# The head of a decoder layer: unused products on TensorE, transposes by row tile, first tokens on VectorE

## The chip, the cores and the metric

The kernel runs on one core of one Trainium2 chip. TensorE (PE) multiplies matrices, VectorE (DVE), ScalarE (ACT) and GpSimd (POOL) do the rest, and SyncE (SP) issues most of the transfers. The metric is the time of one execution in device microseconds (us); several runs are made and their median counts.

## The reference, cut to what matters

One layer of a conditioned hybrid decoder, for 256 prompt tokens of one sequence and 64 sample tokens (eight sequences of eight). Both groups share every weight. The model has 2048 channels. All arithmetic is float32.

```python
mod = jax.nn.silu(c) @ w_ada + b_ada                      # one vector per sequence, 6 x 2048
sh1, sc1, g1, sh2, sc2, g2 = [m[:, None, :] for m in jnp.split(mod, 6, axis=-1)]
h = _rmsnorm(x, norm1_g) * (1 + sc1) + sh1
p = h @ w_in                                              # q, k, v, og, u, ga, gb, alr
...
x = x + g1 * (merged @ w_o)
h2 = _rmsnorm(x, norm2_g) * (1 + sc2) + sh2
gate, up = jnp.split(h2 @ w_gu, 2, axis=-1)
x = x + g2 * ((jax.nn.silu(gate) * up) @ w_down)
```

Nothing of `p` can be computed for a block of 128 channels before that block of `h` exists, and `h` needs x with its channels on the partitions, the reciprocal norm of each token, and the shift and scale (`sh1`, `sc1`) that come from a product of the conditioning vectors with the first third of `w_ada`.

## The kernel before, in words

Tokens lie along the free dimension: T = 320 columns, 256 prompt and 64 sample. Channels lie on the partitions, 16 blocks of 128 (KT = 16), called token tiles below: `xT[k]` is x of block k, `hh[k]` and `hl[k]` the rounded and the remaining part of h. Every weight goes through the same steps: a transfer from memory into a tile `raw` (line 142, three buffers), a rounded copy `whi` on ScalarE (152) and the remainder `wlo` on VectorE (153), and three products for each 128 x 128 block (166 to 168: whi with hh, whi with hl, wlo with hh).

The transfers of weights are issued on SyncE's queue, each pinned behind what was issued before it in the program (`keep_in_program_order` at 144). A queue whose next transfer waits for a buffer holds up all behind it. Other instructions are ordered by a scheduler that works from its own simulation, except where a line pins one behind the instruction traced before it on the same engine.

The head, in the order of the program:

- The conditioning vectors (nine rows) and x are loaded. x comes in three row tiles `xn[0..2]`: 128 + 128 prompt tokens and 64 sample tokens (lines 382 to 388). Small vectors come by GpSimd's queue (392 to 397).
- TensorE transposes the conditioning rows (400; `tr` is line 129), ScalarE and VectorE make silu of them, `scT`.
- For each of the 16 channel blocks three transposes, one from each row tile, fill one PSUM tile, which VectorE or ScalarE copies to `xT[k]` in turn (453 to 462).
- The squares of x are summed on ScalarE (476); a small product on TensorE spreads the reciprocal norm over all partitions, `rx` (478 to 486).
- `HeadJob` computes shift and scale for some channel blocks. Its `load` brings two tiles of `w_ada` (eight buffers), its `burst` multiplies them (`ada_mm`, line 218: four products side by side for each of four channel blocks), its `finish` transposes the result and adds the bias into `mod` (438 to 445, 233, 236). The first job makes them for token tiles 0 and 1 in four bursts.
- `h_unit(k)` makes hh[k] and hl[k]: VectorE works on the prompt columns (490, 497), GpSimd on the sample columns (491 to 493), ScalarE rounds (494, 495).
- The channel blocks are taken in slices (0 to 1, 2 to 3, 4 to 7, 8 to 11, 12 to 15). For each slice all units of the first head and some gates are projected: q, k, v (a pair of 256 columns), u, og, ga, gb and two further gb pairs. Between the units the next slice's work is spread as a list of steps: the spill of xT to memory by GpSimd's queue (503), the next HeadJob's load, its bursts and finish, and its h_units. `proj` (172) loads four blocks of 256 columns at a time, `proj_pair` (199) two blocks of 512.

After the slices the other three heads, the output projection and the feed-forward follow; the change touches nothing of these.

Of the kernel before, what the change touches and what calls it, by code (L numbers as in the profile page):

```python
# [11 lines left out]
F32 = mybir.dt.float32  # L12
F32R = mybir.dt.float32r
I32 = mybir.dt.int32
AF = mybir.ActivationFunctionType
ALU = mybir.AluOpType
# [4 lines left out]
P = 128  # L21
TP, NB, LS = 256, 8, 8
TS = NB * LS
T = TP + TS
D = 2048
KT = D // P
# [10 lines left out]
WB = 5  # L37
AB = 3
SLICES = ((0, 2), (2, 4), (4, 8), (8, 12), (12, 16))
# [41 lines left out]
def body(tc, A):  # L81
# [3 lines left out]
    wp = ctx.enter_context(tc.tile_pool(name="wp", bufs=3))  # L85
# [3 lines left out]
    hp = hcx.enter_context(tc.tile_pool(name="hp", bufs=1, side="right"))  # L89
    acx = ExitStack()  # L90
    pmain = ctx.enter_context(tc.tile_pool(name="pmain", bufs=2, space=PSUM))
# [5 lines left out]
    def nm(s):  # L97
        uid[0] += 1
        return "%s_%d" % (s, uid[0])

    def misc():
        return pmisc.tile([P, 512], F32, tag="m", name=nm("pm"))

    V, S, G, PE = nc.vector, nc.scalar, nc.gpsimd, nc.tensor
# [4 lines left out]
    ident = cst[:, 0:P]  # L109
    ones = cst[:, P:2 * P]  # L110
# [16 lines left out]
    def tr(out, in_):  # L127
        k = in_.shape[0]
        PE.transpose(out, in_, ident[:k, :k])  # L129
# [5 lines left out]
    def raw_chunk(src, nk, nn, pool=None, tag="raw", bufs=3):  # L135

        if pool is None and more:
            more.reverse()
            if more[0] is not None:
                pool, bufs = more[0], 2  # L140
        t = (pool or wp).tile([P, nk, nn], F32, tag=tag, bufs=bufs, name=nm("raw"))
        ins = nc.sync.dma_start(t, src)
        if in_order[0]:
            tc.keep_in_program_order(ins)
        return t
# [7 lines left out]
        V.tensor_sub(lo, raw, hi.bitcast(F32))  # L153
        return hi, lo

    def split_chunk(src, nk, nn):

        raw = raw_chunk(src, nk, nn)
        step = 512 // nn
        for k in range(0, nk, step):  # L160
            hi, lo = split(raw[:, k:min(k + step, nk)])
            for j in range(hi.shape[1]):
                yield k + j, hi[:, j], lo[:, j]
# [6 lines left out]
    def proj(w, col, k0, k1, xh, xl):  # L170

        ps = pmain.tile([P, 2, 512], F32, tag="pm", name=nm("ps"))
        for c0 in range(k0, k1, 4):
            nk = min(4, k1 - c0)
            for j, whi, wlo in split_chunk(w[:, c0:c0 + nk, col:col + 256], nk, 256):
                kt = c0 + j
                for i in range(2):
                    mm3(ps[:, i, :T], whi[:, i * P:(i + 1) * P], wlo[:, i * P:(i + 1) * P],
                        xh[kt], xl[kt], kt == k0, kt == k1 - 1)
            ada_pump()  # L180
        return ps
# [14 lines left out]

    def proj_pair(w, col, k0, k1, xh, xl):

        parts = list(split_chunk(w[:, k0:k1, col:col + 512], k1 - k0, 512))
        for half in range(2):  # L200
            ps = pmain.tile([P, 2, 512], F32, tag="pm", name=nm("ps"))
            for j, whi, wlo in parts:
                kt = k0 + j
                for i in range(2):
                    c = (2 * half + i) * P
                    mm3(ps[:, i, :T], whi[:, c:c + P], wlo[:, c:c + P], xh[kt], xl[kt], kt == k0, kt == k1 - 1)
            yield ps

    wada = A["w_ada"][0].rearrange("(kt p) n -> p kt n", p=P)
    win = A["w_in"][0].rearrange("(kt p) n -> p kt n", p=P)  # L210
# [79 lines left out]
    def modp(sec, kt):  # L290
        return mod[:, sec * KT + kt, 0:1]

    def mods(sec, kt):
        return mod[:, sec * KT + kt, 1:9].unsqueeze(2).broadcast_to([P, NB, LS])

    def s3(ap):
        return ap.rearrange("p (b t) -> p b t", t=LS)

    hh = [hp.tile([P, T], F32R, tag="hh%d" % k, name="hh%d" % k) for k in range(KT)]
    hl = [None] * KT  # L300
# [70 lines left out]
    def units(h):  # L371
        return [("q", 0, OQ + DK * h), ("k", 0, OK_ + DK * h), ("v", 0, OV + DV * h),
                ("v", 1, OV + DV * h + 256), ("u", 0, OU + 256 * h),
                ("og", 0, OOG + DV * h), ("og", 1, OOG + DV * h + 256),
                ("ga", 0, OGA + DV * h), ("ga", 1, OGA + DV * h + 256),
                ("gb", 0, OGB + DV * h), ("gb", 1, OGB + DV * h + 256)]


    with tc.tile_pool(name="head", bufs=1) as xp:
        junk = xp.tile([P, D], F32, name="junk")  # L380
        crow = junk[0:9, :]
        nc.sync.dma_start(crow[0:1, :], A["c_prompt"])
        nc.sync.dma_start(crow[1:9, :], A["c_sample"])
        xn = [xp.tile([P, D], F32, name="xn%d" % i) for i in range(3)]
# [9 lines left out]
        for j, n in enumerate(("norm1_g", "norm2_g", "final_norm_g", "pool_scale")):  # L394
            a = A[n] if n == "final_norm_g" else A[n][0]
            nc.gpsimd.dma_start(vr1[16 * j:16 * j + 16, :], a.rearrange("(r p) -> r p", p=P))
        nc.gpsimd.dma_start(vr1[64:68, :], A["gla_norm_g"][0].rearrange("(r p) -> r p", p=P))
        pt = misc()
        for k in range(KT):
            tr(pt[:, 16 * k:16 * k + 9], crow[:, k * P:(k + 1) * P])  # L400
        csig = xp.tile([P, KT, 9], F32, name="csig")
        crT = pt[:, 0:256].rearrange("p (k r) -> p k r", r=16)[:, :, 0:9]
        S.activation(csig, crT, AF.Sigmoid)
# [5 lines left out]
        class HeadJob:  # L409


            def __init__(self, b0, s):
                self.b0, self.s, self.w, self.nk = b0, s, 64 * s, 8 // s
                self.ps = None
                self.raws = {}
# [34 lines left out]


        xT = []
        for k in range(KT):
            pt = misc()
            for i in range(3):
                n = P if i < 2 else TS
                tr(pt[:, i * P:i * P + n], xn[i][:n, k * P:(k + 1) * P])
            if k < SLICES[0][1]:
                xT.append(xp.tile([P, T], F32, name="xT%d" % k))
            else:  # L460
                xT.append(hp.tile([P, T], F32, tag="hl%d" % k, name="xT%d" % k))
            (S.copy if k % 2 else V.tensor_copy)(xT[k], pt[:, 0:T])

        pt = misc()
        tr(pt[:, 0:96], vr0)
        tr(pt[:, 96:164], vr1)
# [2 lines left out]
        for sec in (1, 4):  # L469
            V.tensor_scalar(bada[:, sec * KT:(sec + 1) * KT], bada[:, sec * KT:(sec + 1) * KT], 1.0, None, op0=ALU.add)  # L470

        ssq = xp.tile([P, 3], F32, name="ssq")
        V.memset(ssq, 1.0)
        for i in range(3):
            n = P if i < 2 else TS
            S.activation(junk[:n], xn[i][:n], AF.Square, accum_out=ssq[:n, i:i + 1])
        S.activation(ssq, ssq, AF.Sqrt, scale=1.0 / D, bias=epst)
        V.reciprocal(ssq, ssq)
        prs = misc()
        dg = xp.tile([P, 3, P], F32, name="dg")  # L480
        for i in range(3):
            n = P if i < 2 else TS
            V.tensor_scalar(dg[:n, i, :n], ident[:n, :n], ssq[:n, i:i + 1], None, op0=ALU.mult)
            PE.matmul(prs[:, i * P:i * P + n], lhsT=ones[:n, :], rhs=dg[:n, i, :n], start=True, stop=True)
        rx = xp.tile([P, T], F32, name="rx")
        V.tensor_copy(rx, prs[:, 0:T])

        def h_unit(k):
            t = xp.tile([P, T], F32, tag="xh", bufs=2, name=nm("xh"))
            V.scalar_tensor_tensor(t[:, 0:TP], xT[k][:, 0:TP], modp(1, k), rx[:, 0:TP], op0=ALU.mult, op1=ALU.mult)  # L490
            G.tensor_tensor(t[:, TP:T], xT[k][:, TP:T], rx[:, TP:T], op=ALU.mult)
            G.tensor_tensor(s3(t[:, TP:T]), s3(t[:, TP:T]), mods(1, k), op=ALU.mult)
            G.tensor_tensor(s3(t[:, TP:T]), s3(t[:, TP:T]), mods(0, k), op=ALU.add)
            S.activation(hh[k][:, 0:TP], t[:, 0:TP], AF.Identity, bias=modp(0, k))
            S.copy(hh[k][:, TP:T], t[:, TP:T])
            hl[k] = hp.tile([P, T], F32R, tag="hl%d" % k, name="hl%d" % k)
            V.scalar_tensor_tensor(hl[k][:, 0:TP], t[:, 0:TP], modp(0, k), hh[k][:, 0:TP].bitcast(F32),
                                   op0=ALU.add, op1=ALU.subtract)
            V.tensor_sub(hl[k][:, TP:T], t[:, TP:T], hh[k][:, TP:T].bitcast(F32))  # L499
# [25 lines left out]
        for h in EARLY_GB:  # L525
            ge = G0()
            ge.gb = merged[h]
            early += [(ge, "gb", i, OGB + DV * h + 256 * i) for i in range(2)]
        for f in HeadJob(0, SLICES[0][1]).steps():
            f()  # L530
        for k in range(SLICES[0][1]):
            h_unit(k)
        for si, (k0, k1) in enumerate(SLICES):
            bg = []
            acc = 0 if si == 0 else 1
# [28 lines left out]
            e = 0  # L564
            while e < len(early):
                ge, kind, i, col = early[e]
# [445 lines left out]
    for ui in range(8):  # L1012
# [4 lines left out]
        for i in range(2):  # L1017
            residual(ps, i, 2 * ui + i, 2)
            k = 2 * ui + i
# [20 lines left out]
    for k in range(KT):  # L1040
        t = f2.tile([P, T], F32, tag="h2", bufs=3, name=nm("h2"))
# [6 lines left out]
                               op0=ALU.add, op1=ALU.subtract)  # L1048
# [4 lines left out]
    parts = ((0, 22), (22, 44))  # L1053
    ada_rate(0.75, 48)
    for pi, (f0, f1) in enumerate(parts):
# [22 lines left out]
        for ui in range(8):  # L1078
            ps = proj(wdn, 256 * ui, f0, f1, ah, al)
            for i in range(2):  # L1080
                k = 2 * ui + i
                residual(ps, i, k, 5)
                if pi == 1:
# [3 lines left out]
                    pt = misc()  # L1087
                    for a in range(3):
                        n = P if a < 2 else TS
                        tr(pt[:n, a * P:(a + 1) * P], xg[:, a * P:a * P + n])  # L1090
                    for a in range(3):
                        n = P if a < 2 else TS
# [5 lines left out]
    pt = misc()  # L1098
    for a in range(3):
        n = P if a < 2 else TS  # L1100
        PE.matmul(pt[:n, 2 * a:2 * a + 2], lhsT=acc2[:, a * P:a * P + n], rhs=ones[:, 0:2], start=True, stop=True)
    rr = fp.tile([P, 64], F32, name="rr")[:, 0:6]
    for a in range(3):
        n = P if a < 2 else TS
# [3 lines left out]
    for a in range(3):  # L1108
        n = P if a < 2 else TS
# [30 lines left out]
```

## Time and profile before

| | |
|---|---|
| median of three runs | 1993.09 us (1992.62 to 1994.77) |
| the profiled execution | 1993.81 us |
| its span, first to last instruction | 1992.0 us |
| granted TensorE clock, mean over the span | 0.991 |
| transfers | 400.83 MB, mean 201 GB/s |
| chain that ended last, by engine | TensorE 93%, transfers 4% |

The profile is one execution. Its timeline has rows of "start, duration, engine, line, operation, written tile and read tiles, shapes, count", merged where the same instruction repeats; brackets hold the idle time of the engine before it and what ended it. PEld are the weight loads of TensorE, which overlap with its products. A view of stretches gives for each the busy time of PE, PEld, DVE, ACT and POOL with the number of instructions, the granted clock, the share of the DMA engines' time and the rate. A view of transfers gives the count, the size of each and the time from issue to landing.

### The profile page before, as it was taken

The numbers are of one execution on the slowest core, as the hardware profiler recorded it, in microseconds if no ns is written. First come the engines' busy times: TensorE is split into PE (matmuls) and PEld (weight loads), VectorE is DVE, ScalarE is ACT, GpSimd is POOL, SyncE is SP. The second block draws the span as 40 slices with busy tenths as digits, with TensorE's granted clock in tenths as the row PEclk, the third lists the DMA queues.
The fourth block names the chain that finished last, engine by engine and source line by source line (L and its number), as shares of the span: only waits on it lengthen the run. The fifth ranks groups of instructions, "written<-read, shape, count | busy, mean of one in ns | idle before, by whom it ended". The sixth has DMA issues, their size and how long they took to land.

```text
span 1992.0 us, 37175 instructions
## 1 busy us (share of the span) xinstructions
PE 1942.7 (98%) x15008; PEld 1848.6 (93%) x15008; DVE 1014.1 (51%) x1881; ACT 819.6 (41%) x1468; POOL 137.5 (7%) x261
## 2 busy tenths in 40 slices
PE   7999999999999999999989999999999999999997
PEld 5789998898999899889979999999999999999997
DVE  2556665574546544664574444344444444444554
ACT  4333374364335333643353333343333434344443
POOL 1112220111011100110030000000000000000000
PEclk9999999999999999999989999999999999999998
DMA  9888754775975787579636666544445544444442
GB/s 296 287 303 271 230 165 147 263 262 187 325 245 174 269 266 234 167 248 339 226 112 223 202 221 193 167 150 143 156 147 151 153 152 148 149 148 149 148 143 90
DMA packets 319598, 400.83 MB, mean 201 GB/s; under 512 B 13529, under 2 KB 259801, under 8 KB 319089
## 3 DMA queue, kind: packets, MB, share of 16 engines
q1 hardware_dynamic: 307154, 358.21, 56.1%
q0 software_dynamic: 12272, 40.25, 5.4%
q8 instruction: 117, 1.92, 0.4%
q14 instruction: 55, 0.45, 0.1%
HBM read 373.96 MB, written 24.67 MB: 200 GB/s over the span
## 4 chain that ended last, share of the span: by engine, by line
PE 93%; DMA 4%; DVE 1%; ACT 1%; issue 1%; SPq 0%; POOL 0%; ACTq 0%; POOLq 0%; DVEq 0%
PE ps L166 27%; PE ps L168 27%; PE ps L167 27%; PE pm L218 5%; PE pm L129 2%; DMA raw<-w_ada 1%; DMA raw<-w_in 1%; DMA raw<-w_o 1%; PE pm L804 1%; PE pm L825 1%; PE pm L773 1%; DMA xn<-x_sample 1%; PE pm L800 0%; PE pm L762 0%; DVE wlo L153 0%
## 5 line engine op out<-in xcount | busy, mean ns | idle before, releaser
L153 DVE TENSOR_TENSOR wlo<-raw,whi 128x512 fp32r<-128x512 f32 x952 | 658.6, 696 | 817.5 <-ACT whi L152 807.5
L152 ACT CAST whi<-raw 128x512 fp32r<-128x512 f32 x952 | 586.3, 621 | 995.4 <-PE ps L167 843.8
L166 PE MATMUL ps<-hh,whi 128*128 128x320 f32 x1408 | 443.3, 315 | 6.5 <-ACT whi L152 3.0
L166 PE MATMUL ps<-h2h,whi 128*128 128x320 f32 x1408 | 437.4, 311 | 5.1 <-ACT h2h L1046 5.1
L168 PE MATMUL ps<-hh,wlo 128*128 128x320 f32 x1408 | 440.4, 313 | 0.1
L167 PE MATMUL ps<-hl,whi 128*128 128x320 f32 x1408 | 438.7, 312 | 0.4 <-DVE hl L499 0.4
L168 PE MATMUL ps<-h2h,wlo 128*128 128x320 f32 x1408 | 435.5, 309 | 0.0
L167 PE MATMUL ps<-h2l,whi 128*128 128x320 f32 x1408 | 435.5, 309 | 0.0
L166 PEld LDWEIGHTS ps<-hh,whi 128*128 128x128 f32 x1408 | 265.6, 189 | 25.6 <-issue 11.8
L168 PEld LDWEIGHTS ps<-hh,wlo 128*128 128x128 f32 x1408 | 265.6, 189 | 7.9 <-issue 5.7
L166 PEld LDWEIGHTS ps<-h2h,whi 128*128 128x128 f32 x1408 | 265.0, 188 | 8.5 <-ACT h2h L1046 6.1
L167 PEld LDWEIGHTS ps<-hl,whi 128*128 128x128 f32 x1408 | 265.7, 189 | 7.5 <-issue 5.9
L167 PEld LDWEIGHTS ps<-h2l,whi 128*128 128x128 f32 x1408 | 264.9, 188 | 0.0
L168 PEld LDWEIGHTS ps<-h2h,wlo 128*128 128x128 f32 x1408 | 264.9, 188 | 0.0
L166 PE MATMUL ps<-ah,whi 128*128 128x320 f32 x704 | 218.7, 311 | 0.0
L168 PE MATMUL ps<-ah,wlo 128*128 128x320 f32 x704 | 217.5, 309 | 0.0
L167 PE MATMUL ps<-al,whi 128*128 128x320 f32 x704 | 217.5, 309 | 0.0
L167 PEld LDWEIGHTS ps<-al,whi 128*128 128x128 f32 x704 | 132.2, 188 | 0.0
L166 PEld LDWEIGHTS ps<-ah,whi 128*128 128x128 f32 x704 | 132.2, 188 | 0.0
L168 PEld LDWEIGHTS ps<-ah,wlo 128*128 128x128 f32 x704 | 132.2, 188 | 0.0
L218 PE MATMUL pm<-raw,scT 128*32 128x128 f32 (+1 forms) x2688 | 104.7, 296 | 4.3 <-DMA raw<-w_ada 4.3
L218 PEld LDWEIGHTS pm<-raw,scT 128*32 128x32 f32 x2688 | 72.0, 112 | 25.3 <-issue 13.6
(279 smaller groups left out, 1538.2 us busy)
## 6 DMA issues: line engine op xcount, KB each, us to landing
raw<-w_ada SPq DMA_DIRECT2D x192, 512.0 KB, 6.1
raw<-w_gu SPq DMA_DIRECT2D x176, 512.0 KB, 3.5
raw<-w_in SPq DMA_DIRECT2D x173, 512.0 KB, 4.3
raw<-w_down SPq DMA_DIRECT2D x80, 512.0 KB, 3.4
S<-state_gla POOLq DMA_DIRECT2D x16, 1024.0 KB, 8.7
o_gs<-S POOLq DMA_DIRECT2D x16, 1024.0 KB, 7.6
raw<-w_o SPq DMA_DIRECT2D x32, 512.0 KB, 5.3
raw<-w_down SPq DMA_DIRECT2D x16, 256.0 KB, 2.5
```

The source lines that it names most:

```text
L129: PE.transpose(out, in_, ident[:k, :k])
L152: S.copy(hi, raw)
L153: V.tensor_sub(lo, raw, hi.bitcast(F32))
L166: PE.matmul(ps, lhsT=whi, rhs=xhi, start=start, stop=False)
L167: PE.matmul(ps, lhsT=whi, rhs=xlo, start=False, stop=False)
L168: PE.matmul(ps, lhsT=wlo, rhs=xhi, start=False, stop=stop)
L218: ins = PE.matmul(ps[32 * j:32 * j + 32, 0:w], lhsT=scT[:, k, :], rhs=raws[j], start=k == 0 if start is None else start, stop=k == KT - 1 ...
L773: PE.matmul(pt, lhsT=E["kdn"][:, s, d * P:(d + 1) * P], rhs=E["vn"][:, s], start=s == 0, stop=s == 1)
L804: PE.matmul(pt[32 * j:32 * j + 32, :], lhsT=qeP[:, d, 4 * gg + j, :], rhs=E["S0", gg, d][:, j], start=False, stop=d == 1, tile_position=(0 ...
L825: PE.matmul(pt, lhsT=kpz[:, gg, j, d * P:(d + 1) * P], rhs=E["vp"][:, gg], start=True, stop=True)
```

## The change

It has five parts, all in the head.

1. *Unused products.* `keep_busy(n)` issues n products of a tile of ones into a PSUM tile that nobody reads, pinned in program order: 12 at the start, 6 after the transposes of the conditioning rows, 12, 12 and 4 after the three row tiles' first transposes, 5 after each of the first three bursts.
2. *Transposes.* Token tiles 0 to 2 are transposed row tile by row tile as these land. The others are transposed between the bursts (tiles 3 to 5 after the first, 6 to 8, 9 to 11, and 12 after the last), and 13 to 15 after the first tokens. All are pinned.
3. *Conditioning.* All loads of the first job are issued at once, the norm's small product stands ahead of the third burst.
4. *First tokens.* `h_first(0)` and `h_first(1)` take the place of `h_unit` for token tiles 0 and 1: the sample columns are computed on VectorE in place of GpSimd, and x times the norm (`xhat`) is made ahead of the modulation. The rounding on ScalarE applies scale and shift itself.
5. *First weights.* The tiles `raw` of q, k, v and u are loaded before the slice begins, and their whi and wlo are pinned at given places among the steps of the first tokens (`EarlySplit`); `split_chunk` hands them out when the unit comes.

```diff
+    class EarlySplit:
+        def __init__(self, raw):
+            n = raw.shape[2]
+            self.raw = raw
+            self.h = wp.tile([P, 512 // n, n], F32R, tag="whi", bufs=WB, name=nm("whi"))
+            self.l = wp.tile([P, 512 // n, n], F32R, tag="wlo", bufs=WB, name=nm("wlo"))
+
+        def hi(self):
+            tc.keep_in_program_order(S.copy(self.h, self.raw))
+
+        def lo(self):
+            tc.keep_in_program_order(V.tensor_sub(self.l, self.raw, self.h.bitcast(F32)))
...
+        if key in ready:
+            k = 0
+            for e in ready.pop(key):
+                for j in range(e.h.shape[1]):
+                    yield k, e.h[:, j], e.l[:, j]
+                    k += 1
+            return
...
+        idle = pmain.tile([P, 2, 512], F32, tag="pm", name=nm("idle"))
+
+        def keep_busy(n):
+
+            for _ in range(n):
+                tc.keep_in_program_order(PE.matmul(idle[:, 0, 0:64], lhsT=ones, rhs=ones[:, 0:64], start=True, stop=True))
+
+        def ptr(out, in_):
+            k = in_.shape[0]
+            tc.keep_in_program_order(PE.transpose(out, in_, ident[:k, :k]))
+
+        keep_busy(12)
         pt = misc()
         for k in range(KT):
-            tr(pt[:, 16 * k:16 * k + 9], crow[:, k * P:(k + 1) * P])
+            ptr(pt[:, 16 * k:16 * k + 9], crow[:, k * P:(k + 1) * P])
+        keep_busy(6)
...
+        def x_trans(k, eng):
             pt = misc()
             for i in range(3):
                 n = P if i < 2 else TS
-                tr(pt[:, i * P:i * P + n], xn[i][:n, k * P:(k + 1) * P])
...
+                ptr(pt[:, i * P:i * P + n], xn[i][:n, k * P:(k + 1) * P])
+            xT.append(x_place(k))
+            (S.copy if eng else V.tensor_copy)(xT[k], pt[:, 0:T])
+
+        job0 = HeadJob(0, SLICES[0][1])
+        for k0 in range(0, KT, 4):
+            job0.load(k0)
...
+        pts = [misc() for _ in range(NX0)]
+        for i in range(3):
+            n = P if i < 2 else TS
+            for k in range(NX0):
+                ptr(pts[k][:, i * P:i * P + n], xn[i][:n, k * P:(k + 1) * P])
+            keep_busy((12, 12, 4)[i])
+        for k in range(NX0):
+            xT.append(x_place(k))
+            V.tensor_copy(xT[k], pts[k][:, 0:T])
...
+        def h_first(k):
+
+            t = xhat[k]
+            S.activation(hh[k][:, 0:TP], t[:, 0:TP], AF.Identity, scale=modp(1, k), bias=modp(0, k))
+            V.tensor_tensor(s3(t[:, TP:T]), s3(t[:, TP:T]), mods(1, k), op=ALU.mult)
+            V.tensor_tensor(s3(t[:, TP:T]), s3(t[:, TP:T]), mods(0, k), op=ALU.add)
+            S.copy(hh[k][:, TP:T], t[:, TP:T])
+            hl[k] = hp.tile([P, T], F32R, tag="hl%d" % k, name="hl%d" % k)
+            V.tensor_scalar(t[:, 0:TP], t[:, 0:TP], modp(1, k), modp(0, k), op0=ALU.mult, op1=ALU.add)
+            V.tensor_sub(hl[k], t, hh[k].bitcast(F32))
...
-        for f in HeadJob(0, SLICES[0][1]).steps():
-            f()
-        for k in range(SLICES[0][1]):
-            h_unit(k)
+        nx = SLICES[0][1]
+        for i, k0 in enumerate(range(0, KT, 4)):
+            if i == 2:
+                x_norm()
+            job0.burst(k0)
+            while len(xT) < (6, 9, 12, 13)[i]:
+                x_trans(len(xT), len(xT) % 2)
+            if i < 3:
+                keep_busy(5)
+        ew = []
+        for kind, i, col in units(0)[:5]:
+            if kind == "v" and i == 1:
+                continue
+            raw = raw_chunk(win[:, 0:nx, col:col + (512 if kind == "v" else 256)], nx, 512 if kind == "v" else 256)
+            ready[col] = [EarlySplit(raw)] if kind != "v" else [EarlySplit(raw[:, j:j + 1]) for j in range(nx)]
+            ew += ready[col]
+        ew[0].hi()
+        job0.finish()
+        h_first(0)
+        ew[0].lo()
+        ew[1].hi()
+        h_first(1)
+        while len(xT) < KT:
+            x_trans(len(xT), 1)
+        for e in ew[1:]:
+            if e is not ew[1]:
+                e.hi()
+            e.lo()
```

`x_norm` holds the three small products of the norm, the copy to `rx` and the products `xhat`; `x_place` chooses where xT[k] lies, as before.

More of the change, by code (lines that the diff above doesn't have):

```diff
@@ L154, in split, with split_chunk @@
         return hi, lo
-    def split_chunk(src, nk, nn):
+    ready = {}
+    class EarlySplit:
[8 more added lines that the diff above has]
+            tc.keep_in_program_order(V.tensor_sub(self.l, self.raw, self.h.bitcast(F32)))
+    def split_chunk(src, nk, nn, key=None):
+        if key in ready:
[5 more added lines that the diff above has]
+            return
         raw = raw_chunk(src, nk, nn)
@@ L174, in proj @@
             nk = min(4, k1 - c0)
-            for j, whi, wlo in split_chunk(w[:, c0:c0 + nk, col:col + 256], nk, 256):
+            for j, whi, wlo in split_chunk(w[:, c0:c0 + nk, col:col + 256], nk, 256, col if w is win else None):
                 kt = c0 + j
@@ L197, in proj_pair @@
     def proj_pair(w, col, k0, k1, xh, xl):
-        parts = list(split_chunk(w[:, k0:k1, col:col + 512], k1 - k0, 512))
+        parts = list(split_chunk(w[:, k0:k1, col:col + 512], k1 - k0, 512, col))
         for half in range(2):
@@ L452, in body, with x_place @@
         xT = []
-        for k in range(KT):
+        NX0 = 3
+        def x_place(k):
+            if k < SLICES[0][1]:
+                return xp.tile([P, T], F32, name="xT%d" % k)
+            return hp.tile([P, T], F32, tag="hl%d" % k, name="xT%d" % k)
+        def x_trans(k, eng):
             pt = misc()
@@ L456, in body @@
                 n = P if i < 2 else TS
-                tr(pt[:, i * P:i * P + n], xn[i][:n, k * P:(k + 1) * P])
[L458 to L462, printed above, removed]
+                ptr(pt[:, i * P:i * P + n], xn[i][:n, k * P:(k + 1) * P])
[4 more added lines that the diff above has]
+            job0.load(k0)
+        ssq = xp.tile([P, 3], F32, name="ssq")
+        V.memset(ssq, 1.0)
+        for i in range(3):
+            n = P if i < 2 else TS
+            S.activation(junk[:n], xn[i][:n], AF.Square, accum_out=ssq[:n, i:i + 1])
+        pts = [misc() for _ in range(NX0)]
+        for i in range(3):
+            n = P if i < 2 else TS
+            for k in range(NX0):
[4 more added lines that the diff above has]
+            V.tensor_copy(xT[k], pts[k][:, 0:T])
         pt = misc()
@@ L470, in body @@
             V.tensor_scalar(bada[:, sec * KT:(sec + 1) * KT], bada[:, sec * KT:(sec + 1) * KT], 1.0, None, op0=ALU.add)
[L472 to L476, printed above, removed]
         S.activation(ssq, ssq, AF.Sqrt, scale=1.0 / D, bias=epst)
@@ L479, in body, with x_norm @@
         prs = misc()
[L480 to L484, printed above, removed]
-        rx = xp.tile([P, T], F32, name="rx")
-        V.tensor_copy(rx, prs[:, 0:T])
+        rx = xp.tile([P, T], F32, name="rx")
+        xhat = []
+        def x_norm():
+            dg = xp.tile([P, 3, P], F32, name="dg")
+            for i in range(3):
+                n = P if i < 2 else TS
+                V.tensor_scalar(dg[:n, i, :n], ident[:n, :n], ssq[:n, i:i + 1], None, op0=ALU.mult)
+                tc.keep_in_program_order(PE.matmul(prs[:, i * P:i * P + n], lhsT=ones[:n, :], rhs=dg[:n, i, :n],
+                                                   start=True, stop=True))
+            V.tensor_copy(rx, prs[:, 0:T])
+            for k in range(SLICES[0][1]):
+                t = xp.tile([P, T], F32, tag="xh", bufs=2, name=nm("xh"))
+                V.tensor_tensor(t, xT[k], rx, op=ALU.mult)
+                xhat.append(t)
+        def h_first(k):
[7 more added lines that the diff above has]
+            V.tensor_sub(hl[k], t, hh[k].bitcast(F32))
         def h_unit(k):
```

## The prediction

> **What bounds the kernel now.** I read the page's first part, then the chain that ended last, then the timeline and the stretches of the first 50 us, where every edit lies.
>
> ```profile
> span 1992.0 us, 37175 instructions
> PE 1942.7 (98%) x15008; PEld 1848.6 (93%) x15008; DVE 1014.1 (51%) x1881; ACT 819.6 (41%) x1468; POOL 137.5 (7%) x261
> ```
>
> TensorE is busy 98% of the span, so time can be won only where it stands idle, runs slowly or does other work than the projections. The change touches the stretch before the first projection. Its timeline before (start, duration, engine, line, count; in brackets the idle time before):
>
> ```profile
> 7.08 1.11 PE L129 MATMUL pm<-cst,xn 128*128 128x128 f32 x4 [1.36 <-DMA xn<-x_prompt]
> 10.61 1.12 PE L129 MATMUL pm<-cst,xn 128*128 128x128 f32 x4 [2.42 <-DMA xn<-x_prompt]
> 12.82 0.69 PE L129 MATMUL pm<-cst,xn 64*128 64x64 f32 x4 [1.09 <-DMA xn<-x_sample]
> 13.77 11.03 PE L129 MATMUL pm<-cst,xn 128*128 128x128 f32 x36 [0.26 <-DVE xT L462]
> 24.94 1.73 PE L484 MATMUL pm<-dg,cst 128*128 128x128 f32 x6
> 26.60 3.66 PE L218 MATMUL pm<-raw,scT 128*32 128x128 f32 x80
> 30.40 1.52 PE L218 MATMUL pm<-raw,scT 128*32 128x128 f32 x48
> 32.99 0.18 DVE L236 TENSOR_TENSOR mod<-mod,vec 128x18 f32<-128x18 f32 x1
> 33.72 0.51 ACT L494 ACTIVATE hh<-xh,mod 128x256 fp32r<-128x256 f32 x1 [0.41 <-DVE xh L490]
> 34.26 0.74 POOL L493 TENSOR_TENSOR xh<-xh,mod 128x64 f32<-128x64 f32 x1
> 35.03 0.24 ACT L495 CAST hh<-xh 128x64 fp32r<-128x64 f32 x1 [0.80 <-POOL xh L493]
> 35.33 0.56 PE L166 MATMUL ps<-hh,whi 128*128 128x320 f32 x2 [2.67 <-ACT hh L495]
> ```
>
> The x transposes wait for the last row tile (12.82), TensorE runs 36 of them for 11.03 us (306 ns each), then all conditioning bursts (to 31.92), and the first projection starts at 35.33. Here is the same sort of work later, from the chain in order of time (start, duration, what):
>
> ```profile
> 51.76 1.01 PE pm L218 x32
> 441.52 1.75 PE pm L129 x16
> 467.52 0.64 PE pm L716 x4
> ```
>
> There a transpose takes 109 ns and a burst product 32 ns; the head's first 80 take 46 ns each. So TensorE runs slowly until some 29 us, though its clock column says 1.00 there, as these stretches show (length, busy time of five engines, clock, DMA share, GB/s):
>
> ```profile
> 12.50:24.50 12.00, 11.42 (x40) 5.96 (x40) 4.56 (x12) 6.38 (x13) 0.00 (x0) 1.00 1.10 350
> 26.50:29.50 3.00, 3.00 (x61) 2.70 (x64) 0.49 (x1) 0.02 (x1) 0.32 (x1) 1.00 0.04 14
> 36.00:39.50 3.50, 3.22 (x12) 3.22 (x13) 1.45 (x4) 0.77 (x2) 2.65 (x6) 0.51 0.96 286
> 39.50:41.00 1.50, 1.50 (x12) 1.45 (x10) 0.00 (x0) 0.48 (x1) 0.00 (x0) 1.00 1.08 373
> 46.00:48.50 2.50, 2.33 (x41) 1.90 (x40) 2.08 (x4) 1.44 (x3) 0.00 (x0) 1.00 1.06 392
> ```
>
> The second row shows DMA with nothing to do; the third a clock of 0.51 for 3.5 us after the 2.67 us of idle time: about 1.7 us lost. [...]
>
> What follows the head is the other bound. SyncE's queue issues the weights in program order:
>
> ```profile
> 28.56 0.92 SPq L142 DMA_DIRECT2D raw<-w_ada  x2
> 31.68 0.37 SPq L142 DMA_DIRECT2D raw<-w_in  x1
> 32.14 2.12 SPq L142 DMA_DIRECT2D raw<-w_ada  x4
> 34.35 1.06 SPq L142 DMA_DIRECT2D raw<-w_in  x1
> ```
>
> The last is the weight of the first output gate (og). In the chain from 40 to 60 us:
>
> ```profile
> 34.35 11.34 DMA raw<-w_in
> 45.77 0.63 ACT whi L152
> ...
> 47.12 0.74 DVE v L355
> 48.00 0.39 PE ps L166
> 48.38 0.15 PE ps L167
> ```
>
> Its 11.34 us are on the chain: it lands at 45.69 behind six w_ada chunks, and og's products start at 48.00. So whatever the head gains, I must ask when this transfer lands after the change.
>
> **The change part by part.**
>
> *The unused products* (42 ahead of the first burst, 15 between bursts). A float32 product of this kind shows as two instructions (L484 issues three, its row shows six). The trace has none with 64 columns; the bounds at full clock are 109 ns (the transpose) and 160 ns (L716, 128 columns), I take 109 as half the columns are streamed; at the slow rate L484 bounds it at 288 ns. The first 24 instructions start at 1 us in idle time and end by 6 to 8 us, at 0.2 to 0.288 each. The rest fill waits for x (the row tiles' first transposes stand at 7.08, 10.61 and 12.82): 24 instructions between row tiles are 2.6 us at full clock, so the last row tile's transposes come at some 14 us and the first burst is reached near 15.5. They cost nothing there, because the first two w_ada chunks land only at about 15.7. That is from the last chunk, less six at 350 GB/s (1.5 us each):
>
> ```profile
> 15.88 1.42 SPq L142 DMA_DIRECT2D raw<-w_ada  x1
> raw<-w_ada SPq DMA_DIRECT2D x1, 512.0 KB, 8.8
> ```
>
> Issued at 15.88, it lands 8.8 later, at 24.7.
>
> *From there to the last burst.* TensorE's work in the new order, at full clock: four bursts of 1.01 = 4.0; nine groups of three transposes at 109 ns = 2.9; 15 unused products = 3.3; the norm's six instructions at 160 ns = 1.0. Sum 11.2, so 15.7 + 11.2 = 26.9. By the data: the last chunk at 24.7 plus the burst, 25.7. One thing moves on a queue: xspill. Its four issues stood behind POOL's work for the first tokens, which goes to VectorE; now nothing of this sort is ahead of them and they can leave when xT exists, at 14 to 17 us:
>
> ```profile
> 36.09 2.22 POOL L503 DMA_DIRECT2D xspill<-xT  x4
> xspill<-xT POOLq DMA_DIRECT2D x4, 160.0 KB, 7.6
> ```
>
> Their 0.65 MB at 350 GB/s are 1.9 us in the middle of the w_ada chunks: 27.6 by the data. I take 27.2 for the last burst's end (bounds 25.7 and 27.6), against 31.92: 4.7 us earlier. The VectorE and ScalarE copies of the transposes lie beside it (in this trace 36 of the 48 took all of 11 us, so none of the copies was late; at the higher rate one pair of copies per 0.7 us is needed, and a copy takes 0.4 to 0.5 on two engines).
>
> *First tokens.* From the burst's end to the modulation 1.25 us stay (31.92 to 33.17). Then before, POOL's last step ended at 35.00 and ScalarE's cast let TensorE go at 35.33: 2.16 us. After, ScalarE's 0.51 and cast of 0.24 remain, with two VectorE operations beside the 0.51 (of 128x64; nearest the row below, 0.21 each), with gaps 0.9. So the first projection comes at 27.2 + 1.25 + 0.9 = 29.3, 6.0 earlier, and the slow 3.5 us may go too (1.7).
>
> ```profile
> 36.54 0.21 DVE L499 TENSOR_TENSOR hl<-xh,hh 128x64 fp32r<-128x64 f32 x1
> 36.97 0.69 DVE L153 TENSOR_TENSOR wlo<-raw,whi 128x512 fp32r<-128x512 f32 x1 [0.22 <-ACT whi L152]
> ```
>
> *The added wait.* Four w_in tiles (q, k, v, u) are now loaded ahead, into three buffers, and the wlo of q is pinned behind hl of the first token tile on VectorE. So u's load waits for q's buffer until 29.2 + 0.6 (hl) + 0.7 (wlo) = 30.5. It stands on SyncE's queue; behind it wait six w_ada chunks and og. Before, the first two of these left at 28.56, and u at 31.68. The queue thus restarts 2 us later than before, though TensorE is 6 us ahead. From issue to landing u takes 3.2 us in the trace:
>
> ```profile
> raw<-w_in SPq DMA_DIRECT2D x1, 256.0 KB, 3.2
> ```
>
> u is there at 33.8; TensorE reaches it near 38: VectorE has q's wlo at 30.5, the second tile's steps at 31.8 (1.3 more, as the first's) and k's wlo at 32.5; the 12 products that are then left end at 34.3, and v's 24 at 0.15 take 3.5. So no stall there. Then 7 transfers of 512 KB: 9.4 us at 392 GB/s, 10.5 at 350. og lands at 43.2 to 44.3. TensorE has done u (1.7) and the burst (1.0) by some 41 and waits. og's first product starts 0.75 after the landing (whi alone; the evacuation of v that stood ahead of it at 47.1 to 47.9 is long done): 44.0 to 45.0, against 48.00. The gain is 3.0 to 4.0, I take 3.5. Behind it the weights come from buffers that TensorE's own progress frees, so that later stages move as a whole and nothing more is won or lost.
>
> **Sum.** 6.0 at the first projection, 3.5 after the wait for og. The profiled execution took 1993.8 (1.8 around the span of 1992.0) and would take 1990.3; on the median of the runs shown, 1993.09, that is 1989.6. What a measurement can tell from no change is 0.2%, 4.0 us: this forecast lies just inside.
>
> **The rivals.**
>
> *The head's gain is kept whole.* If og lands by 40 (q's wlo running before hl, or u's load not in front), the 6.0 and the slow stretch's 1.7 are won: 1985.4. For it speaks that TensorE's 98% leave little else; against it the chain's 11.34 us and the program order of the queue. 0.15.
>
> *The clock falls while TensorE waits for og.* [...] 0.2. [...]
>
> *The unused products do not raise the clock early.* Then they are work ahead of x: 84 instructions at 0.22 (109 ns doubled) to 0.288 are 18 to 24 us, the first burst starts at 22 or later instead of 15.7, and all the rest moves: at least 5 us slower than before by og, 1998, up to 2003. It decides if the fast rate is not there when the second row tile lands. [...] Against it: L484 and the bursts, also float32, raised the rate in 4 us. 0.12.
>
> *The loads eat it all.* If the spills still stand at 36 us and the w_ada rate is the 286 to 338 GB/s around them, og lands where it did: 1993.1. 0.08.
>
> **How the numbers follow.** Forecast 1989.6 with 0.45 (own range 1988.3 to 1991), rivals as given. Faster by over 0.2% (under 1989.1): the whole gain's 0.15 and some 0.17 of the forecast, 0.32. Slower: 0.12. The same: 0.56. The range 1986.0 to 1994.0 leaves out the slower rival and about half of the whole gain, 0.2 in all.
>
> **What would show it.** Right: transposes near 0.11 us from the second row tile on; last burst's end near 27, first projection near 29; u's load at 30 to 31 on SyncE's queue after some 3 us of idle DMA; a TensorE wait of about 3 us ending with og's landing at 43 to 44; equal distances afterwards. Wrong: transposes at 0.3 us beyond 12 us, a first projection after 32, or og without a wait ahead of it.

## The result, and the profile after

The changed kernel is slower: 2011.72 us (median of four runs, 2006.02 to 2017.82) against 1993.76 us for the kernel before beside it (1992.62 to 1994.77). The ratio is 1.0097, with a 95% interval of 1.0077 to 1.0117. The forecast was 1989.6 with a range up to 1994.0. The profiled execution took 2014.67 us. Its page begins:

```profile
span 2012.9 us, 37419 instructions
PE 1971.0 (98%) x15130; PEld 1877.2 (93%) x15130; DVE 1015.8 (50%) x1885; ACT 820.0 (41%) x1468; POOL 134.6 (7%) x255
```

The span grew by 20.9 us and TensorE's busy time by 28.3, so in sum the lost time is time in which TensorE is busy, not idle. The timeline of TensorE in the head shows which (start, duration, line, count; L427 are the unused products, L431 the pinned transposes, L242 the bursts, L190 the first projection):

```profile
1.06 5.38 PE L427 MATMUL idle<-cst 128*128 128x64 f32 x24 [1.06 <-DVE cst L111]
...
11.43 5.22 PE L427 MATMUL idle<-cst 128*128 128x64 f32 x24
16.44 0.85 PE L431 MATMUL pm<-cst,xn 128*128 128x128 f32 x3
17.08 5.22 PE L427 MATMUL idle<-cst 128*128 128x64 f32 x24
22.23 0.58 PE L431 MATMUL pm<-cst,xn 64*128 64x64 f32 x3
...
24.91 1.94 PE L242 MATMUL pm<-raw,scT 128*32 128x128 f32 x32
26.78 2.81 PE L431 MATMUL pm<-cst,xn 128*128 128x128 f32 x9
29.52 2.39 PE L427 MATMUL idle<-cst 128*128 128x64 f32 x10
...
47.28 1.94 PE L242 MATMUL pm<-raw,scT 128*32 128x128 f32 x32
...
50.25 1.73 PE L431 MATMUL pm<-cst,xn 128*128 128x128 f32 x9
53.36 1.15 PE L190 MATMUL ps<-hh,whi 128*128 128x320 f32 x2 [1.39 <-ACT hh L556]
```

Up to 49 us everything runs at the slow rate: nine transposes take 2.81 us, and a burst of 32 takes 1.94 where the one at 75.97 takes 1.08. The unused products never bring the fast rate; the nine transposes at 50.25 are the first to have it. No bracket stands between 1.06 and 50.25: TensorE works through its stream without idling, and the unused products are part of it. They take 0.22 us per instruction, 5.2 us between row tiles where the forecast had 2.6. The first projection comes at 53.36 instead of 35.33, 18.0 us later.

The transfers wait with it. SyncE's queue, and the stretches (length, five engines, clock, DMA share, GB/s):

```profile
16.88 37.99 SPq L142 DMA_DIRECT2D raw<-w_in  x4
54.98 6.43 SPq L142 DMA_DIRECT2D raw<-w_ada  x6
61.51 1.78 SPq L142 DMA_DIRECT2D raw<-w_in  x1
```

```profile
0.00:26.00 26.00, 24.94 (x143) 24.31 (x146) 3.64 (x17) 9.05 (x10) 5.97 (x17) 1.00 0.97 307
26.00:36.00 10.00, 10.00 (x75) 6.59 (x67) 0.98 (x2) 1.21 (x3) 0.54 (x1) 1.00 0.18 72
36.00:60.00 24.00, 22.59 (x148) 18.02 (x147) 8.75 (x22) 7.64 (x18) 0.70 (x1) 0.93 0.17 54
65.20:70.80 5.60, 0.00 (x0) 0.00 (x0) 0.01 (x1) 0.66 (x2) 0.00 (x0) 0.68 1.08 368
70.80:74.00 3.20, 3.19 (x12) 3.19 (x13) 1.29 (x2) 0.48 (x1) 0.00 (x0) 0.50 0.89 285
```

The four tiles of q, k, v and u are one row of the queue that lasts until 54.87: u's load, the last of them, waits for q's buffer. Behind it stand the six w_ada chunks and og, so from 30 to 54 us almost nothing is moved (1 GB/s). Then TensorE stands idle for 5.6 us until og's weight is there (fourth row) and starts it at half clock (fifth row). The clock column says 1.00 in the first two rows, though the bursts in them take 1.94 us: as in the kernel before, where it said 1.00 beside transposes of 306 ns.

The chain, in order of time:

```profile
61.51 8.53 DMA raw<-w_in
70.14 0.63 ACT whi L152
70.81 0.63 PE ps L190
...
492.45 0.64 PE pm L813 x4
```

Og's first product is at 70.81 instead of 48.00, 22.8 us later. The last row is a step whose row of before the prediction shows (467.52, L716): it comes 24.9 us later. Nearly the whole loss is thus there at 71 us; later it shrinks by 4 us to the 20.9 of the span.

### The profile page after: what moved, and what is told of

Read it like the earlier page. It is cut to its first block, busy times and chain, and to the rows that moved or that the text cites. A ratio compares the mean times of both kernels' runs of the same rounds, so it can differ in the third digit from the quotient of the medians.

```text
span 2012.9 us, 37419 instructions
## 1 busy us (share of the span) xinstructions
PE 1971.0 (98%) x15130; PEld 1877.2 (93%) x15130; DVE 1015.8 (50%) x1885; ACT 820.0 (41%) x1468; POOL 134.6 (7%) x255
## 3 DMA queue, kind: packets, MB, share of 16 engines
q8 instruction: 118, 1.93, 0.4%
## 4 chain that ended last, share of the span: by engine, by line
PE 93%; DMA 3%; ACT 1%; DVE 1%; issue 1%; SPq 0%; POOL 0%; ACTq 0%; POOLq 0%; DVEq 0%
PE ps L190 27%; PE ps L192 27%; PE ps L191 27%; PE pm L242 5%; DMA raw<-w_in 2%; PE idle L427 1%; PE pm L129 1%; DMA raw<-w_ada 1%; PE pm L901 1%; PE pm L922 1%; PE pm L431 1%; PE pm L870 1%; PE pm L897 0%; PE pm L859 0%; DVE wlo L153 0%
## 5 line engine op out<-in xcount | busy, mean ns | idle before, releaser
L190 PE MATMUL ps<-hh,whi 128*128 128x320 f32 x1408 | 444.2, 316 | 10.9 <-ACT whi L152 8.8
L190 PE MATMUL ps<-h2h,whi 128*128 128x320 f32 x1408 | 437.8, 311 | 5.1 <-ACT h2h L1143 5.1
L190 PEld LDWEIGHTS ps<-hh,whi 128*128 128x128 f32 x1408 | 266.1, 189 | 29.0 <-ACT whi L152 14.1
L190 PEld LDWEIGHTS ps<-h2h,whi 128*128 128x128 f32 x1408 | 265.3, 189 | 8.0 <-ACT h2h L1143 5.6
L190 PE MATMUL ps<-ah,whi 128*128 128x320 f32 x704 | 218.7, 311 | 0.0
L190 PEld LDWEIGHTS ps<-ah,whi 128*128 128x128 f32 x704 | 132.2, 188 | 0.0
L242 PE MATMUL pm<-raw,scT 128*32 128x128 f32 (+1 forms) x2688 | 106.0, 298 | 2.0 <-DMA raw<-w_ada 2.0
L242 PEld LDWEIGHTS pm<-raw,scT 128*32 128x32 f32 x2688 | 72.2, 112 | 23.4 <-issue 14.5
```

Source lines behind the costliest of these rows:

```text
L190: PE.matmul(ps, lhsT=whi, rhs=xhi, start=start, stop=False)
L242: ins = PE.matmul(ps[32 * j:32 * j + 32, 0:w], lhsT=scT[:, k, :], rhs=raws[j], start=k == 0 if start is None else start, stop=k == KT - 1 ...
```

## The experiments

The theory was: the unused products do not raise the clock, and so they are plain work on the path. The reason that went with it, that half of each is a weight load, was shown by no run. The rivals were: something else in the new order is slow (then the loss stays without them), and: products with constant operands cannot raise the clock (then wider ones would not either).

**Without the unused products (e1).**

```
-            for _ in range(n):
-                tc.keep_in_program_order(PE.matmul(idle[:, 0, 0:64], lhsT=ones, rhs=ones[:, 0:64], start=True, stop=True))
+            return
```

> All unused products left out, everything else as in the changed kernel. Theory A (they are plain work: the chain holds 27 us of them, and they never raised the clock): transposes still at 0.3 us, last burst's end near 33, first projection near 37 instead of 53.4, total 1995 to 2000. Rival B (what delays the head is the pinned order, the early weights or the wait for og, not the unused products): first projection after 45 and total over 2005.

Measured: 1994.73 us (1991.61 to 2000.78, seven runs), 1.0018 (1.0006 to 1.0031) of the kernel before. That is 17.0 us under the changed kernel (15.7 by the ratios): the unused products are nearly all of its loss. All else in the change together is still slightly slower than before. Its first projection and og's first product:

```profile
35.59 0.93 PE L190 MATMUL ps<-hh,whi 128*128 128x320 f32 x2 [1.39 <-ACT hh L554]
...
52.26 0.64 PE L190 MATMUL ps<-hh,whi 128*128 128x320 f32 x1 [4.51 <-ACT whi L152]
```

The first projection comes when it did before (35.33), but og's first product 4.3 us later than the 48.00 of before, behind a wait of 4.51 us. So the rival has a part too, a small one: the new order delays og.

**512 columns, a quarter as many (e2), and 128 columns, two thirds as many (e3).**

```
-            for _ in range(n):
-                tc.keep_in_program_order(PE.matmul(idle[:, 0, 0:64], lhsT=ones, rhs=ones[:, 0:64], start=True, stop=True))
e2:
+            for _ in range((n + 2) // 4):
+                tc.keep_in_program_order(PE.matmul(idle[:, 0, :].rearrange("p (a b) -> p a b", a=4), lhsT=ones,
+                                                   rhs=ones.unsqueeze(1).broadcast_to([P, 4, P]), start=True, stop=True))
e3:
+            for _ in range((2 * n + 1) // 3):
+                tc.keep_in_program_order(PE.matmul(idle[:, 0, 0:P], lhsT=ones, rhs=ones, start=True, stop=True))
```

> The same time of unused products, but each streams 512 columns of ones and there are a quarter as many. Theory A (what counts for the clock is the time in which columns stream; with 64 columns half of each instruction is the weight load): the fast rate (transposes near 0.11 us) comes by 8 us, first projection at 29 to 31, a TensorE wait for og of about 3 us, total 1988 to 1992. Rival C (products of a constant tile of ones do not count, whatever their length): transposes at 0.3 us to beyond 40, total 2006 to 2018 as the changed kernel.

> [...] Theory A: between the other two; the clock may rise early in some executions and not in others, so times from 1989 to 2015 with a wide spread, and in the profiled one either transposes at 0.11 us by 10 us or at 0.3 to beyond 30. Rival C: as the changed kernel, 2006 to 2018.

Measured: 2001.09 us (1998.32 to 2001.3; 1.0042, 1.0026 to 1.0059) and 2000.77 (1999.02 to 2002.49; 1.0045, 1.0030 to 1.0060). TensorE's timeline with 512 columns, and then with 128:

```profile
1.06 5.47 PE L427 MATMUL idle<-cst 128*128 128x512 f32 x6 [1.06 <-DVE cst L111]
6.47 1.15 PE L432 MATMUL pm<-cst,junk 9*128 9x9 f32 x16
```

```profile
1.06 3.78 PE L427 MATMUL idle<-cst 128*128 128x128 f32 x16 [1.06 <-DVE cst L111]
4.77 1.87 PE L431 MATMUL pm<-cst,junk 9*128 9x9 f32 x16
...
16.18 1.08 PE L242 MATMUL pm<-raw,scT 128*32 128x128 f32 x32
17.20 1.78 PE L431 MATMUL pm<-cst,xn 128*128 128x128 f32 x9
...
27.76 1.08 PE L242 MATMUL pm<-raw,scT 128*32 128x128 f32 x32
...
32.62 0.41 PE L190 MATMUL ps<-hh,whi 128*128 128x320 f32 x1 [1.39 <-ACT hh L556]
```

After 5.4 us of 512-column products the sixteen small transposes take 1.15 us, the fast rate, where they took 1.87. With 128 columns they are still slow at 4.77, but the bursts from 16.18 on are fast. So constant operands do raise the clock, and that rival is dead. In a stretch as long (5.4 us) and as unbroken, the number of columns per instruction made the difference. The totals were a miss: 1988 to 1992 was expected of e2 and a wide spread of e3, whose four runs lie within 3.5 us. So a second thing is settled: with the clock up early, the change is still slower than before by 0.4%. In e3 the first burst (16.18) and last burst (end at 28.84) are near the forecast's 15.5 and 27.2, but the first projection comes at 32.62, not at 29.3. ScalarE's timeline says why:

```profile
30.13 1.00 ACT L504 COPY xT<-pm 128x320 f32<-128x320 f32 x2 [0.93 <-PE pm L431]
31.02 1.09 ACT L553 ACTIVATE hh<-xh,mod 128x256 fp32r<-128x256 f32 x2
32.02 0.41 ACT L504 COPY xT<-pm 128x320 f32<-128x320 f32 x1
32.32 0.25 ACT L556 CAST hh<-xh 128x64 fp32r<-128x64 f32 x1
```

Three copies of transposed x and the rounding of the second token tile run ahead of the cast that the first projection waits for. The scheduler was free to place them there. But 32.62 is still 2.7 us ahead of before, so the 0.4% are lost behind it. Og's first product comes at 49.43, 1.4 us later than before, and after that wait the products run at half rate up to 53.6 us (one per 0.27 us, then one per 0.15). At the step of 467.52 e3 is 8.0 us behind: between 60 and 215 us its chain passes through five transfers of w_in, that of before through one. Where each part of the 8.0 arises was not followed.

**Without u among the early loads (e4, on top of e2).**

```
-        for kind, i, col in units(0)[:5]:
+        for kind, i, col in units(0)[:4]:
```

> As the kernel with 512 columns, and u is no longer among the weights loaded ahead (q, k, v only), so three buffers serve three tiles and the w_ada chunks of the next slice stand ahead of u on SyncE's queue. Theory A with the wait for og as forecast: w_ada leaves before 28, og lands by 41, TensorE's wait for it under 1.5 us, total 2 to 4 us less than with u ahead. Rival D (og is bound by the rate of the transfers, not by when the queue restarts): same time within 1 us.

Measured: 1994.05 us (1991.82 to 1999.17, ten runs; 1.0013, 1.0003 to 1.0022), by the ratios about 6 us better than e2, and the intervals do not meet. So loading u early, in front of the next slice's w_ada, costs that much:

```profile
17.00 3.24 SPq L142 DMA_DIRECT2D raw<-w_in  x3
20.35 3.98 SPq L142 DMA_DIRECT2D raw<-w_ada  x2
35.86 0.37 SPq L142 DMA_DIRECT2D raw<-w_in  x1
```

Two of the six w_ada chunks are now issued at 20 us, ahead of u, and the stretch from 26 to 36 us moves 175 GB/s where e2's moves 66. The steps came later than forecast: the other four chunks leave only behind u, og lands at 47.9 in place of 41, and its first product is at 48.68 (e2: 51.75).

**The weights of q and k split ahead of the first tokens (f1, on top of e3), and ScalarE's order pinned too (f2), the latter without unused products (f3) and with those ahead of the first burst only (f4).** What stands behind # is a note, not code.

```
+        for e in ew[:2]:                     # f1: in place of ew[0].hi(); ew[0].lo() after h_first(0); ...
+            e.hi()
+            e.lo()
         job0.finish()
...
+            if k > 12:                       # f2: copies of the last x tiles; the second ACTIVATE alike
+                tc.keep_in_program_order(ins)
...
-            if i < 3:                        # f4 (f3: keep_busy returns at once)
-                keep_busy(5)
```

> As the kernel with 128-column unused products (first projection 32.6, og landed 48.7), with hi and lo of q and k placed ahead of the conditioning's last step instead of behind the first tokens, so that their raw buffers come free as soon as the weights land. Theory Q (og lands 15 us after u's load leaves SyncE's queue, and u waits for q's buffer): u leaves near 29 instead of 33.8, og lands at 43 to 45, og's first product by 45.5 instead of 49.4, total 3 to 5 us lower than e3_128 (2000.8). Rival D (og is bound by the rate or by what stands on the engines): og still at 48 or later, same total within 1 us.

> f1_split_early, and the ScalarE copies of token tiles 13 to 15 and the rounding of the second token tile are pinned behind the first tile's cast. First projection 1 to 1.5 us earlier than in f1_split_early. Theory Q: TensorE waits that much longer for og and the total is the same within 1 us. Rival E (the first projection sets the pace): total 1 us or more lower.

> f2_pins without any unused product. Last burst near 31.8 at the slow rate as in e1_none, first projection near 34.5, u leaves near 30 instead of 36.7, og lands near 45 instead of 51.5. Theory Q: total 4 to 6 us lower than e1_none (1994.7), so 1989 to 1991. Rival F (the raised clock is worth more than the loads): 3 us or more slower than f2_pins.

> f2_pins without the unused products between the bursts. If real bursts alone hold the clock (1.0 us in each 2.8): last burst's end 2.6 us earlier, near 26.5, bound then by the landing of the last w_ada chunk, first projection near 29.5; by theory Q og comes about as in f2_pins and the total is within 1.5 us of it. If transposes between bursts let the clock fall: transposes back to 0.3 us from some 20 us on, last burst after 29.

Measured, in this order: 1995.76 (1992.06 to 2000.12, nine runs; 1.0011, 0.9998 to 1.0025), 1994.06 (1.0013, 0.9998 to 1.0027), 1994.97 (1.0011, 0.9996 to 1.0027) and 1993.59 us (1.0010, 0.9993 to 1.0026), the last three with ten runs each. Against e3 they win some 0.3%; none can be told from the kernel before. First projections come at 34.98, 31.88, 32.31 and 31.34 us, og's first products at 47.76, 45.57, 46.34 and 44.53. Two expectations failed. In f1 u's load left at 31.6 in place of 29 and og landed at 47.0 in place of 43 to 45, though the total fell as forecast. F3 was to gain 4 to 6 us on e1 from its earlier queue; og's first product is 5.9 us earlier, but the medians differ by 0.2 us (f3 the higher) and the intervals of the ratios overlap. So an earlier og by itself did not make the whole measurably faster.

The head itself is much better in f4. Its queue, stretches and chain:

```profile
17.70 12.19 SPq L142 DMA_DIRECT2D raw<-w_in  x4
29.99 5.43 SPq L142 DMA_DIRECT2D raw<-w_ada  x6
```

```profile
14.00:28.00 14.00, 11.75 (x165) 7.82 (x163) 4.93 (x17) 4.99 (x11) 2.12 (x4) 1.00 1.05 358
26.00:36.00 10.00, 8.80 (x68) 6.87 (x68) 6.78 (x18) 5.77 (x14) 0.42 (x1) 0.83 0.72 233
36.00:60.00 24.00, 22.79 (x249) 20.63 (x248) 9.35 (x16) 11.50 (x19) 0.00 (x0) 1.00 0.87 292
```

```profile
35.52 8.27 DMA raw<-w_in
...
103.74 8.91 DMA raw<-w_in
130.10 7.61 DMA raw<-w_in
192.49 6.81 DMA raw<-w_in
201.91 8.20 DMA raw<-w_in
...
466.49 0.64 PE pm L814 x4
```

U's load leaves by 29.9, og lands at 43.8 and its first product is at 44.53, 3.5 us ahead of before, which is the forecast's 3.0 to 4.0. But 3.5 us at 44 us are 1.0 us at 466.49 (467.52 before). The chain between 100 and 210 us passes through four transfers of w_in; in the kernel before it passes through none there. The lead is spent on waits for weights. And f2 against f3, the same kernel with and without working unused products, differ by nothing that shows: in this order an early fast clock is worth less than the measurement can tell. The pair is a weak test, though, because in f3's profiled execution the fast rate came by 24 us without them (the norm's six products at 23.96 take 1.07 us, e1's 1.84), and its first projection is only 0.4 us behind f2's.

**The next slice's w_ada ahead of u (g1, on f4; g4, the same without unused products).**

```
+        job1 = HeadJob(SLICES[1][0], SLICES[1][1] - SLICES[1][0])
...
+            if kind == "u":
+                job1.load(0)
```

> f4_no_mid, and the first two w_ada chunks of the next slice are issued ahead of u's load on SyncE's queue, as in the kernel before; their buffers have been free since the first burst. Theory Q (the transfers stand idle from 29 us until q's buffer frees u's load, and all behind it waits): the queue has no gap after v, og lands at 40.5 to 42 instead of 43.8, og's first product near 42; total 2 to 3 us under f4_no_mid, at 1989 to 1991, about 0.1 to 0.2% under the kernel before. Rival G (after 50 us the loads of the next slices are the bound and eat any lead): og earlier as said, total within 1 us of f4_no_mid.

> g1_w_ada_first without any unused product. By theory Q the unused products are worth little once the loads are in order: og lands within 1.5 us of g1_w_ada_first, total within 1.5 us of it. Rival F (the raised clock matters): 3 us or more slower.

Measured: 1994.19 (1989.78 to 1999.57, twelve runs; 1.0009, 0.9998 to 1.0020) and 1993.39 us (1990.57 to 1998.7, eleven runs; 1.0001, 0.9992 to 1.0010). A miss: og lands at 44.55 in g1, not earlier than in f4. The two chunks do leave at 22.9, but in the profiled execution TensorE ran at the slow rate from the burst at 24.34 to some 31.5 (nine transposes at 25.95 took 2.81 us, the burst at 28.69 took 1.93), q's remainder came late and u's load left only at 32.7. Og's first product (46.42) then waited for v's evacuation on ScalarE as well. Again the kernel without unused products is not the slower one, and this pair says more than f2 and f3: in g4's profiled execution the rate stayed slow to some 35 us (three transposes at 33.10 took 0.99 us), the first projection came at 37.06 and og's first product at 49.29, 5.7 and 4.8 us behind f4's (and 2.9 behind g1's, where 1.5 was expected), yet its ratio to the kernel before is not above f4's.

**The kernel before, with 128-column unused products at its start only (g2).**

```
+        keep_busy(8)                # 128 columns each
         pt = misc()
         for k in range(KT):
             tr(pt[:, 16 * k:16 * k + 9], crow[:, k * P:(k + 1) * P])
+        keep_busy(12)
```

> The kernel before with nothing but unused products of 128 columns: 8 at the start and 12 after the conditioning rows' transposes, which end about when the first x row tile is transposed. The transposes of x follow for 9 to 11 us without any other product. If transposes keep the clock (they count as busy): all at 0.11 to 0.19 us, bursts from 20 to 22 us instead of 26.6, first projection 4 us earlier. [...] Total within 3 us of the kernel before either way.

Measured: 1989.94 us (1985.81 to 1995.57, ten runs), 0.9983 of the kernel before (0.9974 to 0.9993). By the medians that is 3.9 us, a little more than the 3 us allowed for. This is the only version whose interval lies below the kernel before. The margin is small: the kernel before itself had medians from 1992.44 to 1993.85 beside the three groups of experiments. Its timeline and stretches:

```profile
6.57 4.88 PE L402 MATMUL idle<-cst 128*128 128x128 f32 x24
11.29 0.60 PE L129 MATMUL pm<-cst,xn 128*128 128x128 f32 x4
...
14.54 9.27 PE L129 MATMUL pm<-cst,xn 128*128 128x128 f32 x36 [0.40 <-DVE xT L470]
...
34.72 0.90 PE L166 MATMUL ps<-hh,whi 128*128 128x320 f32 x2 [3.15 <-ACT hh L503]
```

```profile
10.70:17.40 6.70, 5.16 (x35) 3.37 (x33) 1.87 (x4) 4.88 (x8) 0.00 (x0) 1.00 1.06 301
17.60:27.70 10.10, 10.10 (x68) 6.50 (x71) 2.99 (x9) 3.87 (x8) 0.32 (x1) 0.50 0.97 322
27.80:34.50 6.70, 3.40 (x94) 2.67 (x86) 4.01 (x13) 2.41 (x6) 1.80 (x4) 1.00 0.82 255
```

The fast rate is there by 11.29 (four transposes in 0.60 us, 1.11 before); the clock falls at 17.5, in the middle of the transposes, and comes back with the bursts. The 36 transposes take 9.27 instead of 11.03 us and the first projection comes 0.6 us earlier. The fall comes 6 us after the last unused product: in this run nine microseconds of transposes without a gap did not keep the clock up. The head's 0.6 us do not make up 3.9 us of median. In the profiled execution the lead grows from 0.9 us at 467 us to about 3 at the w_ada wait near 690 and is 1.9 at the end. F4's goes the same way (1.0, 3.7, 1.6) though its median gains nothing, so the profile does not show why g2 wins.

## Why the prediction was wrong, point by point

- *The failed step* is "24 instructions between row tiles are 2.6 us at full clock" and "They cost nothing there". They ran at 0.22 us each, 5.2 us between row tiles, so that the last row tile's transposes were at 22.23 instead of 14 and the first burst at 24.91 instead of 15.5. Left out (e1), they give 17.0 us back. The reason given for the fast rate, that other float32 products had raised it in 4 us, does not carry over to products of 64 columns: with more columns it does come, by 6.47 us in e2 and by 16.18 in e3.
- *The rival was there, and under-priced.* "The unused products do not raise the clock early" had 0.12 and the first burst "at 22 or later", which came true. Its price of 5 to 10 us counted the delay of the first burst alone. The bursts, transposes and unused products behind it ran slowly too: 24.3 us from the first burst's start to the last one's end where the forecast had 11.2. And SyncE's queue stood still all that time. That half of an unused product's time is a weight load, as theory A of e2 has it, no run shows: in the changed kernel the 24 weight loads from 1.06 on take 5.19 us beside the 5.38 of their products. The streaming share as estimated from e2 and e3 stands in the last section.
- *Transposes at full clock were mis-sized*: a group of three was put at 0.33 us and takes 0.57 (nine in 1.71, e3, from 17.20 to 18.91).
- *First tokens were mis-sized*: from the last burst's end to the first projection 2.15 us were forecast; 4.1 were measured after the change and 3.8 in e3, whose timeline shows the ScalarE copies of the last token tiles, for which this step had no term, ahead of the cast.
- *The queue was right.* U's load was put 1.2 us behind the first projection; it leaves 1.1 behind (54.5 after 53.36). From there to og's landing 12.7 to 13.8 us were forecast and 15.5 measured (54.5 to 70.04); from landing to product 0.75 and 0.77.
- *The clock during og's wait* was a rival with 0.2, and it came true as well: the idle 5.6 us are followed by 3.2 us at 0.50. The 2.67 us of idle time ahead of the slow 3.5 us of before lie in a longer stretch: from 31.92 to 35.33 TensorE ran one transpose alone (0.33 us). How long TensorE must be idle for the clock to fall, no run shows.
- *"Later stages move as a whole"* holds for the changed kernel within 4 us in 23. It does not hold for the small leads on which the forecast's sign rested: f4 has the forecast's lead at og and loses most of it by 467 us. So 1989.6 would probably not have been reached even with the clock as forecast.

Where each version stood against the kernel before, in its one profiled execution (us, plus is later), and what its transfers had moved by 60 us:

| | first projection | og's first product | step of 467.52 | end of the span | MB by 60 us |
|---|---|---|---|---|---|
| before | 0 | 0 | 0 | 0 | 16.7 |
| after | +18.0 | +22.8 | +24.9 | +20.9 | 10.0 |
| e1 | +0.3 | +4.3 | +4.9 | +1.0 | 15.6 |
| e2 | -0.9 | +3.8 | +8.1 | +7.4 | 15.8 |
| e3 | -2.7 | +1.4 | +8.0 | +6.9 | 16.1 |
| e4 | -0.6 | +0.7 | +3.9 | +4.0 | 15.9 |
| f1 | -0.3 | -0.2 | +6.8 | +6.3 | 16.4 |
| f2 | -3.4 | -2.4 | +0.8 | +0.6 | 17.2 |
| f3 | -3.0 | -1.7 | +0.2 | +0.6 | 17.0 |
| f4 | -4.0 | -3.5 | -1.0 | -1.6 | 17.4 |
| g1 | -0.8 | -1.6 | +5.2 | +2.7 | 16.2 |
| g2 | -0.6 | -1.3 | -0.9 | -1.9 | 17.1 |
| g4 | +1.7 | +1.3 | +2.8 | -0.8 | 16.1 |

Except for the changed kernel, where og stands in the head says little about the end. The four versions that had moved 17 MB or more by 60 us are within 1 us of before at 467 us or ahead, and those with 15.6 to 16.4 are 2.8 to 8.1 behind; but there is no order among these (g4 and e3 have the same 16.1), and the kernel before itself has 16.7. That early bytes are the cause was not tested by itself: a fourth weight buffer, which might free the queue without touching TensorE, was not tried. One execution is not the median either: f1's is the slowest of its nine.

It stays open, too, what raises the clock, and when. In the changed kernel the norm and a burst, 3.6 us of products without a gap from 38.64 on, did not raise it; the rate rose only behind the burst at 47.28. Without unused products TensorE is busy for 15.75, 15.80 and 15.67 of the first 26 us in e1, f3 and g4, and the fast rate came by 24 us in f3, near 30 in e1 and near 35 in g4. And runs of the changed kernel spread over 12 us where the four of before beside them spread over 2; beside the later experiments before spread over 3 to 11 us itself, so this spread is not the change's alone. At which later waits the runs part was not followed.

## What to carry to other kernels

Work that is put into an in-order stream to keep the clock up is free only if it does keep it up: try products with more columns (here those of 64 did not bring the fast rate in 49 us, those of 512 and 128 did by 6.47 in e2 and 16.18 in e3), and look at the duration of the next real instruction rather than at the clock column, which said 1.00 beside bursts of 1.94 us. Before a head is made shorter for the compute engine, look at what its transfers do: a load pinned ahead of others that waits for a buffer freed by the last step of the head holds up the whole queue (1 GB/s from 30 to 54 us here), and a lead in compute can be spent again where the next stages wait for weights, as in f4.

## What was not expected of the hardware

An unused product instruction takes 0.221 us with 64 columns (24 from 1.06 to 6.37), 0.232 with 128 (16 from 1.06 to 4.77) and 0.90 with 512 (6 from 1.06 to 6.47), all at the slow rate. From 128 to 512 columns that is 1.74 ns per column, so by this estimate the array streams for about 0.11 of the 0.221 us at 64 columns, for 0.22 of the 0.232 at 128 and for nearly all at 512. The first kind did not raise the clock in some 49 us; with the second the fast rate was there by 4.54 us in f4 (its sixteen small transposes take 1.15 us) and by 11.3 us in g2, with the third by 6.5 us in e2. Being busy in the profile, 24.94 of the first 26 us after the change, did not bring the fast rate by itself, nor did single rows of 5.38 and 5.22 us without a gap. That the share of time in which columns stream decides is the author's explanation; it fits these runs, but no run varies it with all else held.
